# One level of Strassen's products in the two channel mixers of a decoder trunk in fp32

## The chip, the cores and the metric

One core of one Trainium2 chip runs the whole trunk in a single launch. The engines are TensorE (PE: matrix products into PSUM; its weight loads are listed as PEld), VectorE (DVE), ScalarE (ACT), GpSimd (POOL) and SyncE (SP), which here only issues transfers. The metric is the time of one execution in microseconds, the median of three runs.

## What is computed

A trunk of two layers over 512 tokens of width 1024. Layer 0 has a chunked gMLP mixer, layer 1 a gated linear recurrence; each is followed by the same channel mixer, a gated ConvFFN with inner width 3072. All in float32.

```
def conv_ffn(h, w_up, conv_w, conv_b, w_down):
    up = causal_dwconv(h @ w_up, conv_w, conv_b)
    gate, val = jnp.split(up, 2, axis=-1)
    return (jax.nn.gelu(gate) * val) @ w_down

def reference(x, ...):
    for i in range(DEPTH):
        h = rms_norm(x, norm_mix[i])
        ...
        x = x + mixer_a(...)          # layer 0; mixer_b in layer 1
        h = rms_norm(x, norm_ffn[i])
        x = x + conv_ffn(h, f_w_up[i], f_conv_w[i], f_conv_b[i], f_w_down[i])
    return rms_norm(x, norm_final)
```

`w_up` is 1024 x 6144 (3072 gate columns, 3072 value columns), `w_down` 3072 x 1024, the convolution has three causal taps over the tokens.

## The kernel before

**Layout.** Everything is feature-major: a tile has 128 features on the partitions and the 512 tokens along the free dimension. x stays in SBUF (`xall`, eight such rows, `xs[k]`). `out` is written transposed.

**Precision.** Every fp32 operand of a product is split into two parts in the format fp32r, hi (a rounded copy, made by ScalarE) and lo (the rest, a subtraction on VectorE), and each product of two tiles is three matmuls: hi·hi, hi·lo and lo·hi (`mm3`, lines 99 to 103). The splits of the weights stand in `split` (lines 85 to 91), with raised priority.

**Products.** `block` (lines 106 to 118) fills four PSUM banks, one for each of four blocks of 128 output features. It walks over the inner dimension in chunks of 256: a chunk is 512 KB of weights (128 x 2 x 512), loaded by SP into one of three `raw` buffers, split into one of three `hi` and one of three `lo` buffers, and multiplied in 2 x 4 x 3 = 24 matmuls of 512 columns. `hooks` put the norm's statistics between chunks; the norm's scale `rbc` is applied to the product's output.

**The channel mixer** (`conv_ffn`, lines 450 to 478). The up product runs in 12 groups of four chunks; a group gives two 128-feature tiles of the gate and the two value tiles that belong to them. Each of these four is multiplied by `rbc` out of PSUM (line 468), goes through three taps (`conv`, lines 442 to 448: one on ScalarE, two on VectorE), the gate tile through gelu, and the two are multiplied on VectorE (line 473) and split by `to_parts` into one of 24 kept pairs. The down product follows, two blocks of 12 chunks: `project` (adds to x, prepares the next norm) in layer 0, `project_out` (final norm, output by halves of the tokens) in layer 1. That makes 48 + 24 = 72 chunks of 24 matmuls in a mixer.

**Order.** The tile framework sets the order on each engine when the program is built, by readiness in its own model and by priority; within an engine instructions then run in that order. GpSimd has 19 instructions in the whole program: constants, four selections that cut the triangle of the spatial weights (line 397), and powers (`rsqrt_mean`, lines 210 to 213, and line 175).

Of the kernel before, what the change touches and what calls it, by code (L numbers as in the profile page):

```python
# [8 lines left out]
F32 = mybir.dt.float32  # L9
# [11 lines left out]
AG = 8  # L21
# [9 lines left out]
# Columns of the packed per-channel vectors.  # L31
# [13 lines left out]
def trunk(ctx: ExitStack, tc: tile.TileContext, xT, vecs, a_w_in, a_w_sT, a_b_s, a_w_out,  # L45
# [5 lines left out]
    yp = ctx.enter_context(tc.tile_pool(name="yp", bufs=24))  # L51
    wk = ctx.enter_context(tc.tile_pool(name="wk", bufs=7))
# [4 lines left out]

    def work(name="w"):
        return wk.tile([P, S], F32, tag="w", name=name)

    def work_r(name="wr"):
        return wk.tile([P, S], F32R, tag="w", name=name)

    def yhi(name="yh"):
        return yp.tile([P, S], F32R, tag="yh", name=name)

    def ylo(name="yl"):
        return yp.tile([P, S], F32R, tag="yl", name=name)

    # Activations whose tables differ, in the order of the program.  # L70
# [13 lines left out]
    # A chunk of a weight: 1024 values a partition, in two parts that add up to it exactly.  # L84
# [20 lines left out]
    # Feature-major product: one PSUM tile for each of four blocks of 128 output features.  # L105
    def block(kt, loader, acts, name, hooks={}):
        pss = [psum(f"{name}{m}") for m in range(4)]
        for kc in range(kt // 2):
            hi, lo = loader(kc)
            last = kc == kt // 2 - 1  # L110
            order = [(k, m) for m in range(4) for k in range(2)] if last else [(k, m) for k in range(2) for m in range(4)]
            for k, m in order:
                kk = 2 * kc + k
                w = (hi[:, k, m * P:(m + 1) * P], lo[:, k, m * P:(m + 1) * P])
                mm3(pss[m], w, acts[kk], kk == 0, kk == kt - 1)
            for hook in hooks.get(kc, ()):
                hook()
# [22 lines left out]
    # Keeps the tensor engine's clock up while the first loads are under way.  # L140
# [19 lines left out]
    # log of the sigmoid, by log1p(u) = 2 atanh(u / (2 + u)) with u = exp(-|lambda|)  # L160
# [36 lines left out]
    def norm_input(k, gain, ts=slice(None)):  # L197
        nc.scalar.activation(xh[k][:, ts], xs[k][:, ts], AF.Copy, scale=gain)  # L198
# [429 lines left out]
```

## Time and profile before

| | us |
|---|---|
| median of three runs | 1341.12 |
| the runs | 1341.08 to 1341.90 |
| span of the profiled execution | 1339.3 |
| PE busy in it | 1329.0 |
| DVE / ACT / POOL busy | 802.6 / 554.0 / 12.0 |
| transfers: mean busy share of the 16 engines, bytes | 29.7%, 129 MB |

The span runs from the first to the last instruction of the program. Busy times are unions of an engine's instructions; matmuls overlap, so the distance between their starts tells what one costs, not the listed duration. A row of a timeline has the start, the length, the engine, the source line, the operation, the tile written and the tiles read; "x3" means that so many equal instructions in a row are merged.

### The profile page before, as it was taken

How to read it: one execution, taken by the hardware profiler on the slowest of the kernel's cores; microseconds unless marked ns; L12 is line 12 of the kernel's file. 1: busy time of each engine (PE TensorE's matmuls, PEld its weight loads, DVE VectorE, ACT ScalarE, POOL GpSimd, SP SyncE). 2: the span in 40 equal slices, each digit the busy share in tenths (PEclk: the TensorE clock that was granted, in tenths of full speed). 3: DMA queues.
4: the chain of work that ended last, by engine and by line, in shares of the span. 5: the costliest groups of instructions: out<-in, count | busy, mean ns of one | idle time of the engine just before them, and what ended most of it. 6: DMA issues, size and time to landing. Idle time of an engine off the chain costs nothing.

```text
span 1339.3 us, 15007 instructions
## 1 busy us (share of the span) xinstructions
PE 1329.0 (99%) x5862; PEld 1082.5 (81%) x5862; DVE 802.6 (60%) x1104; ACT 554.0 (41%) x743; POOL 12.0 (1%) x20
## 2 busy tenths in 40 slices
PE   9999999999999999999999999999999999999997
PEld 7888888888888888888888888888888888888886
DVE  7227775446767575724247799944676757572325
ACT  6455332333434343423233669633343434342322
POOL 1000000000000000000000000000000000000000
PEclk9999999999999999999999999999999999999999
DMA  6333222232222222232233323232222222223221
GB/s 230 94 94 109 80 79 94 94 95 94 94 95 90 94 90 92 94 105 98 94 94 95 95 79 95 97 108 94 95 94 95 90 94 90 92 93 105 99 79 64
DMA packets 96328, 129.19 MB, mean 96 GB/s; under 512 B 5888, under 2 KB 61184, under 8 KB 96256
## 3 DMA queue, kind: packets, MB, share of 16 engines
q1 hardware_dynamic: 96112, 128.22, 29.7%
q8 instruction: 46, 0.75, 0.2%
q14 instruction: 26, 0.21, 0.1%
q10 hardware_dynamic: 144, 0.00, 0.0%
HBM read 126.11 MB, written 2.10 MB: 96 GB/s over the span
## 4 chain that ended last, share of the span: by engine, by line
PE 98%; issue 0%; DMA 0%; DVE 0%; ACT 0%; DVEq 0%; POOLq 0%; POOL 0%
PE f L101 13%; PE f L102 13%; PE f L103 13%; PE fd0p L102 3%; PE fd0p L103 3%; PE fd0p L101 3%; PE fd1p L101 3%; PE fd1p L102 3%; PE fd1p L103 3%; PE u L101 2%; PE v L362 2%; PE v L363 2%; PE u L103 2%; PE u L102 2%; PE v L364 2%; PE aop L101 2%
## 5 line engine op out<-in xcount | busy, mean ns | idle before, releaser
L446 DVE SCALAR_TENSOR_TENSOR cv<-up,vt,cv 128x511 f32<-128x511 f32 (+1 forms) x192 | 140.8, 745 | 22.2 <-ACT cv L444 21.3
L444 ACT ACTIVATE cv<-up,vt 128x512 f32<-128x512 f32 x96 | 77.7, 812 | 77.3 <-DVE up L468 77.3
L468 DVE TENSOR_TENSOR up<-f,rbc 128x512 f32<-128x512 f32 x96 | 65.4, 683 | 0.2 <-issue 0.2
L473 DVE TENSOR_TENSOR cv<-cv 128x512 f32<-128x512 f32 x48 | 33.0, 688 | 1.0
L472 ACT ACTIVATE cv<-cv 128x512 f32<-128x512 f32 x48 | 30.2, 629 | 5.5 <-DVE cv L446 3.3
L198 ACT ACTIVATE xh<-xall,vt 128x512 fp32r<-128x512 f32 x24 | 17.2, 719 | 23.8 <-DVE xall L250 23.8
L422 DVE SCALAR_TENSOR_TENSOR sv<-sv,vt,bs 128x256 f32<-128x256 f32 x32 | 14.9, 477 | 19.1 <-PE sv L419 19.1
L207 ACT ACTIVATE sq<-xall 128x512 f32<-128x512 f32 (+1 forms) x37 | 21.7, 586 | 9.8 <-DVE xall L262 9.8
L446 DVE SCALAR_TENSOR_TENSOR xb<-xr,vt,xb 128x511 f32<-128x511 f32 (+2 forms) x36 | 25.5, 744 | 0.1
L208 DVE TENSOR_TENSOR acc<-acc,sq 128x512 f32<-128x512 f32 (+1 forms) x37 | 23.8, 642 | 2.0 <-ACT sq L207 1.9
L199 DVE SCALAR_TENSOR_TENSOR xl<-xall,vt,xh 128x512 fp32r<-128x512 f32 x24 | 17.9, 748 | 5.2 <-ACT xh L198 4.8
L213 POOL TENSOR_TENSOR rc<-ms,mhalf 128x4 f32<-128x4 f32 (+1 forms) x6 | 5.4, 905 | 1233.5 <-DVE ms L212 1233.5
L418 PE MATMUL sv<-ws,vh 128*128 128x256 f32 x64 | 15.4, 324 | 0.0
L424 DVE SCALAR_TENSOR_TENSOR sv<-sv,vt 128x256 f32<-128x256 f32 x32 | 15.0, 480 | 0.4
L419 PE MATMUL sv<-ws,vl 128*128 128x128 f32 x64 | 14.2, 222 | 0.0
L559 DVE TENSOR_TENSOR_SCAN hs<-riyh,sq 128x512 f32<-128x512 f32 x12 | 14.0, 1205 | 0.0
L76 ACT ACT_TABLE_LOAD x10 | 12.8, 1283 | 0.1
L419 PEld LDWEIGHTS sv<-ws,vl 128*128 128x128 f32 x64 | 12.2, 191 | 0.5
L418 PEld LDWEIGHTS sv<-ws,vh 128*128 128x128 f32 x64 | 12.1, 188 | 0.5
L437 ACT ACTIVATE u<-u 128x512 f32<-128x512 f32 x16 | 9.4, 625 | 7.1 <-DVE u L436 7.1
L444 ACT ACTIVATE xb<-xr,vt 128x512 f32<-128x512 f32 x12 | 9.8, 814 | 6.1 <-DVE xr L492 6.1
L388 DVE SCALAR_TENSOR_TENSOR vl<-vr,rv,vh 128x512 fp32r<-128x512 f32 x16 | 10.9, 747 | 1.9 <-ACT vh L387 1.9
(2590 smaller groups left out, 4210.9 us busy)
## 6 DMA issues: line engine op xcount, KB each, us to landing
xall<-xT SPq DMA_DIRECT2D x8, 256.0 KB, 5.0
outT<-o SPq DMA_DIRECT2D x8, 256.0 KB, 2.4
av00raw<-a_w_in SPq DMA_DIRECT2D x2, 256.0 KB, 3.7
av01raw<-a_w_in SPq DMA_DIRECT2D x2, 256.0 KB, 4.9
av02raw<-a_w_in SPq DMA_DIRECT2D x2, 256.0 KB, 5.7
av03raw<-a_w_in SPq DMA_DIRECT2D x2, 256.0 KB, 5.2
bs<-a_b_s SPq DMA_DIRECT2D x1, 512.0 KB, 6.0
av10r<-a_w_in SPq DMA_DIRECT2D x1, 512.0 KB, 6.5
```

The costliest lines, as they stand in the source:

```text
L101: nc.tensor.matmul(ps, wh, xh, start=first, stop=False)
L102: nc.tensor.matmul(ps, wh, xl, start=False, stop=False)
L103: nc.tensor.matmul(ps, wl, xh, start=False, stop=last)
L362: nc.tensor.matmul(pss[c], xh[kk][:, ts], hi[:, k, :], start=kk == 0, stop=False)
L363: nc.tensor.matmul(pss[c], xh[kk][:, ts], lo[:, k, :], start=False, stop=False)
L364: nc.tensor.matmul(pss[c], xl[kk][:, ts], hi[:, k, :], start=False, stop=kk == KD - 1)
L418: nc.tensor.matmul(ps[:, i], vh[:, ds_], w, start=True, stop=False)
L444: nc.scalar.activation(dst, src, AF.Identity, scale=col(wname, woff + last * wstep), bias=col(cname, coff))
L446: nc.vector.scalar_tensor_tensor(dst[:, i:], src[:, :S - i], col(wname, woff + (last - i) * wstep), dst[:, i:], op0=ALU.mult, op1=ALU.add)
L468: nc.vector.tensor_tensor(upt, pss[2 * half + j], rbc, op=ALU.mult)
L472: nc.scalar.activation(ts[0], ts[0], AF.Gelu_apprx_tanh)
L473: nc.vector.tensor_tensor(ts[1], ts[0], ts[1], op=ALU.mult)
```

## The change

Each channel mixer's products are computed with one level of Strassen's scheme (seven products in place of eight), over quarters: the inner dimension is taken in pairs of 128-row blocks, the output features in two halves (gate and value for the up product; the lower and the upper 512 features of the width for the down product), and the tokens in two halves of 256.

- A chunk is again 512 KB of weights, four quarters of 128 x 256. `weight_sums` makes four sums of quarters in place (on GpSimd: one instruction of 512 elements and two of 256) and splits the seven combinations into two halves `j` of 7 x 128 columns, so two hi parts (ScalarE) and two lo parts (VectorE) of 896 elements in a chunk. There are three `hi` and three `lo` buffers as before, now of 7 x 128 columns, and two `raw` buffers (three before).
- `input_sums` makes the same kind of sums of the product's input (three GpSimd instructions), one cast of 1792 elements and one subtraction of 1792; for x once in a mixer per pair of rows (`prepare`, where gain and `rbc` now go into the input), for y in each group (`finish`).
- `seven` multiplies a chunk in 7 x 2 x 3 = 42 matmuls of 256 columns into seven of the eight PSUM banks.
- A group's seven banks are put together in `shared` and `up`: two copies on ScalarE, five instructions on VectorE (each reads one PSUM bank), two on GpSimd. The product of gate and value moves from VectorE to GpSimd.
- The down product runs in four chunks of the inner dimension, after the groups 3, 6, 8 and 11 (3, 3, 2 and 4 pairs, each for two halves of the output), and is added to x each time: four GpSimd instructions and seven on VectorE per product.
- The first group (`up_plain`, q = 0) keeps the old form, while the norm's statistics are made.
- The output is no longer sent by halves: the final norm follows the last product as a whole.
- SBUF pools are opened and closed by phase; x's parts `xparts` and six of the y tiles share a pool `top`; the first recurrent block takes its chunks in the order 0, 2, 1, 3. Comments are gone.

```
-    yp = ctx.enter_context(tc.tile_pool(name="yp", bufs=24))
-    wk = ctx.enter_context(tc.tile_pool(name="wk", bufs=7))
+    top = ctx.enter_context(tc.tile_pool(name="top", bufs=2))
...
+    PRODUCTS = ((1, 0, 0), (2, 2, 1), (6, 5, 5), (7, 3, 4), (5, 4, 3), (4, 1, 6), (3, 6, 2))
+    def weight_sums(src, name):
+        raw = wp.tile([P, 8, 256], F32, tag="raw", name=f"{name}r", bufs=2)
+        for k in range(2):
+            nc.sync.dma_start(raw[:, 2 * k:2 * k + 2], src[:, k])
+        parts = []
+        with tc.high_priority(HIGH):
+            nc.gpsimd.tensor_tensor(raw[:, 4:6], raw[:, 1:3], raw[:, 0:1].broadcast_to([P, 2, 256]), op=ALU.add)
+            nc.gpsimd.tensor_tensor(raw[:, 6], raw[:, 1], raw[:, 5], op=ALU.add)
+            nc.gpsimd.tensor_tensor(raw[:, 7], raw[:, 3], raw[:, 6], op=ALU.add)
+            for j in range(2):
+                cs = slice(j * P, (j + 1) * P)
+                hi = wp.tile([P, 7, P], F32R, tag="hi", name=f"{name}h{j}", padded_shape=[P, 8, P])
+                lo = wp.tile([P, 7, P], F32R, tag="lo", name=f"{name}l{j}", padded_shape=[P, 8, P])
+                nc.scalar.copy(hi, raw[:, 1:8, cs])
+                nc.vector.tensor_tensor(lo, raw[:, 1:8, cs], hi.bitcast(F32), op=ALU.subtract)
+                parts.append((hi, lo))
+        return parts
+    def input_sums(raw, dst):
+        nc.gpsimd.tensor_tensor(raw[:, 3:5], raw[:, 0:3:2], raw[:, 7:8].broadcast_to([P, 2, HS]), op=ALU.subtract)
+        nc.gpsimd.tensor_tensor(raw[:, 5], raw[:, 3], raw[:, 2], op=ALU.add)
+        nc.gpsimd.tensor_tensor(raw[:, 6], raw[:, 5], raw[:, 1], op=ALU.subtract)
+        hi, lo = dst[:, :, 0:HS], dst[:, :, HS:S]
+        nc.scalar.copy(hi, raw[:, 0:7])
+        nc.vector.tensor_tensor(lo, raw[:, 0:7], hi.bitcast(F32), op=ALU.subtract)
+    def seven(pairs, weight, name):
+        banks = {b: psum(f"{name}m{b}").rearrange("p (j t) -> p j t", j=2) for b, _, _ in PRODUCTS}
+        for n, (q, x) in enumerate(pairs):
+            parts = weight_sums(weight(q), f"{name}{q}")
+            first, last = n == 0, n == len(pairs) - 1
+            for b, w, i in PRODUCTS:
+                for j in range(2):
+                    hi, lo = parts[j]
+                    for m, (wt, xt) in enumerate(((lo, x[:, i, 0:HS]), (hi, x[:, i, 0:HS]), (hi, x[:, i, HS:S]))):
+                        nc.tensor.matmul(banks[b][:, j], wt[:, w], xt, start=first and j == 0 and m == 0,
+                                         stop=last and j == 1 and m == 2, skip_group_check=True)
+        return banks
+    def shared(banks, name):
+        e1, u2, u3 = (etile(f"{name}{t}") for t in ("e1", "u2", "u3"))
+        nc.scalar.copy(e1, banks[1])
+        nc.vector.tensor_tensor(u2, banks[6], e1, op=ALU.subtract)
+        nc.vector.tensor_tensor(u3, u2, banks[7], op=ALU.subtract)
...
+        def finish(q, gate, val):
+            nc.scalar.activation(gate, gate, AF.Gelu_apprx_tanh)
+            raw = yraw(f"yr{q}")
+            for j, place in enumerate(places(raw)):
+                nc.gpsimd.tensor_tensor(place, halves(gate[:, j]), halves(val[:, j]), op=ALU.mult)
...
+        def up(q):
...
+                nc.vector.tensor_tensor(val[:, :, 0:HS], banks[2], e1, op=ALU.add)
+                e5 = etile(f"f{q}e5")
+                nc.scalar.copy(e5, banks[5])
+                nc.gpsimd.tensor_tensor(gate[:, :, HS:S], u3, e5, op=ALU.subtract)
+                nc.gpsimd.tensor_tensor(e5, u2, e5, op=ALU.subtract)
+                nc.vector.tensor_tensor(gate[:, :, 0:HS], u3, banks[4], op=ALU.subtract)
+                nc.vector.tensor_tensor(val[:, :, HS:S], banks[3], e5, op=ALU.subtract)
...
+        top_pairs = (2, 3, 6, 7, 9, 10)
+        up_plain(0)
+        for q in range(1, NF // 2):
+            up(q)
+            if q in (3, 6, 8):
+                down({3: [0, 1, 2], 6: [3, 4, 5], 8: [6, 7]}[q], None)
+        down([8, 9, 10, 11], next_norm)
```

How the order changes is seen at three places. In the names, `f04m5` is bank 5 of layer 0's group 4, `f043h0` and `f043l0` the hi and lo part, half 0, of that group's chunk 3, and `x73` the sums of x for pair 3; without buffer numbers `f051l` is a lo part of group 5, chunk 1, `f5u` an eviction tile, `cg` and `cv` gate and value after the taps. Line numbers of the change are those of the changed file.

VectorE, before, one group of the up product (`up` is the scaled product, `cv` the taps, `fy` the parts of y):

```order
L90 TENSOR_TENSOR fu080l<-fu080r,fu080h 128x1024
L90 TENSOR_TENSOR fu081l<-fu081r,fu081h 128x1024
L468 TENSOR_TENSOR up<-f_3424,rbc 128x512
L446 SCALAR_TENSOR_TENSOR cv<-up,vt,cv 128x511
L468 TENSOR_TENSOR up<-f_3426,rbc 128x512
L446 SCALAR_TENSOR_TENSOR cv<-up,vt,cv 128x510
L468 TENSOR_TENSOR up<-f_3425,rbc 128x512
```

VectorE, after, from the end of group 5 to the next group's second chunk:

```order
L428 TENSOR_TENSOR f053l_4130<-f053r,f053h_4129 128x896
L428 TENSOR_TENSOR f060l_4228<-f060r,f060h_4227 128x896
L428 TENSOR_TENSOR f060l_4232<-f060r,f060h_4231 128x896
L469 TENSOR_TENSOR f5u_4178<-f05m_3946,f5e_4177 128x512
L543 TENSOR_TENSOR uv_4176<-f05m_3945,f5e_4177 128x2x256
L470 TENSOR_TENSOR f5u_4179<-f5u_4178,f05m_3947 128x512
L548 TENSOR_TENSOR ug_4175<-f5u_4179,f05m_3949 128x2x256
L549 TENSOR_TENSOR uv_4176<-f05m_3950,f5e_4184 128x2x256
L402 SCALAR_TENSOR_TENSOR cg_4190<-ug_4175,vt,cg_4190 128x511
L428 TENSOR_TENSOR f061l_4284<-f061r,f061h_4283 128x896
```

Where one lo part of 1024 stood per chunk there are now two of 896, and both lo parts of the next group's first chunk stand ahead of the five evictions.

GpSimd, after, in the same group (before, it has nothing in this stretch):

```order
L422 TENSOR_TENSOR f052r<-f052r 128x256
L511 TENSOR_TENSOR yr_3935<-cg_3920,cv_3927 128x2x256
L420 TENSOR_TENSOR f053r<-f053r 128x512
L511 TENSOR_TENSOR yr_3935<-cg_3920,cv_3927 128x512
L421 TENSOR_TENSOR f053r<-f053r 128x256
L434 TENSOR_TENSOR yr_3935<-yr_3935 128x512
L422 TENSOR_TENSOR f053r<-f053r 128x256
L435 TENSOR_TENSOR yr_3935<-yr_3935 128x256
```

The sums of the weights and of y are interleaved; there are 660 such additions and products in the program, 324 of 512 elements and 336 of 256.

TensorE, after, the end of a chunk and the start of the next group (a chunk before is eight times `hi`, `hi`, `lo` with 512 columns):

```order
L458 MATMUL f04m5_3678<-x73_2446,f043l1_3860 128x256
L458 MATMUL f04m5_3678<-x73_2446,f043h1_3859 128x256 x2
L458 MATMUL f04m4_3679<-x73_2446,f043l0_3856 128x256
L458 MATMUL f04m4_3679<-x73_2446,f043h0_3855 128x256 x2
L458 MATMUL f04m4_3679<-x73_2446,f043l1_3860 128x256
L458 MATMUL f04m4_3679<-x73_2446,f043h1_3859 128x256 x2
L458 MATMUL f04m3_3680<-x73_2446,f043l0_3856 128x256
L458 MATMUL f04m3_3680<-x73_2446,f043h0_3855 128x256 x2
L458 MATMUL f04m3_3680<-x73_2446,f043l1_3860 128x256
L458 MATMUL f04m3_3680<-x73_2446,f043h1_3859 128x256 x2
L458 MATMUL f05m1_3944<-x70_2419,f050l0_3958 128x256
```

Half 0 is used for the last time three matmuls before a chunk's end, and the next chunk's half 1 takes over its buffer.

## Rows read from the trace of the kernel before

**Rows 1.** The page: span, busy time by engine, chain that ended last.

```profile
span 1339.3 us, 15007 instructions
...
PE 1329.0 (99%) x5862; PEld 1082.5 (81%) x5862; DVE 802.6 (60%) x1104; ACT 554.0 (41%) x743; POOL 12.0 (1%) x20
...
PE 98%; issue 0%; DMA 0%; DVE 0%; ACT 0%; DVEq 0%; POOLq 0%; POOL 0%
```

**Rows 2.** Stages: both channel mixers, what follows, and one up group.

```profile
core 0: us, PE busy (x) PEld busy (x) DVE busy (x) ACT busy (x) POOL busy (x), PEclk, DMA share, GB/s
288.50:690.30 401.80, 401.80 (x1739) 326.38 (x1738) 229.72 (x293) 148.35 (x185) 1.01 (x1) 1.00 0.29 95
924.70:1328.50 403.80, 403.80 (x1798) 330.14 (x1797) 231.19 (x303) 150.48 (x193) 1.70 (x2) 1.00 0.27 88
1328.50:1339.30 10.80, 1.92 (x11) 1.23 (x10) 5.00 (x10) 0.93 (x2) 0.70 (x1) 0.70 0.57 195
...
309.00:331.40 22.40, 22.40 (x97) 17.99 (x97) 14.95 (x21) 9.33 (x12) 0.00 (x0) 1.00 0.29 94
```

**Rows 3.** Timeline of PE, start and length in us: 512 columns, then 256.

```profile
309.99 0.40 PE L103 MATMUL f<-xh,fu003l 128*128 128x512 f32 x1
310.22 0.40 PE L101 MATMUL f<-xh,fu003h 128*128 128x512 f32 x1
310.46 0.39 PE L102 MATMUL f<-xl,fu003h 128*128 128x512 f32 x1
...
1317.06 0.28 PE L101 MATMUL fd1p<-fy20h,fd1w110h 128*128 128x256 f32 x1
1317.18 0.28 PE L102 MATMUL fd1p<-fy20l,fd1w110h 128*128 128x256 f32 x1
1317.30 0.28 PE L103 MATMUL fd1p<-fy20h,fd1w110l 128*128 128x256 f32 x1
```

**Rows 4.** Groups of VectorE, 309 to 579 us: count, busy us, mean ns, idle before.

```profile
L446 DVE SCALAR_TENSOR_TENSOR cv<-up,vt,cv 128x511 f32<-128x511 f32 x48 | 35.7, 746 | 10.6 <-ACT cv L444 10.6
L468 DVE TENSOR_TENSOR up<-f,rbc 128x512 f32<-128x512 f32 x48 | 32.7, 683 | 0.0
L473 DVE TENSOR_TENSOR cv<-cv 128x512 f32<-128x512 f32 x24 | 16.5, 688 | 0.5
L90 DVE TENSOR_TENSOR fu032l<-fu032r,fu032h 128x1024 fp32r<-128x1024 f32 x1 | 1.2, 1226 | 0.0
```

**Rows 5.** Timeline of GpSimd and VectorE at 75 us.

```profile
75.51 0.41 POOL L397 TENSOR_SCALAR_AFFINE_SELECT wsm<-wsr 128x256 f32<-128x256 f32 x1 [45.12 <-DMA wsr<-a_w_sT]
75.87 1.39 POOL L397 TENSOR_SCALAR_AFFINE_SELECT wsm<-wsr 128x256 f32<-128x256 f32 x1
77.22 0.40 POOL L397 TENSOR_SCALAR_AFFINE_SELECT wsm<-wsr 128x256 f32<-128x256 f32 x1
75.60 1.40 DVE L90 TENSOR_TENSOR av32l<-av32r,av32h 128x1024 fp32r<-128x1024 f32 x1 [4.38 <-ACT av32h L89]
```

**Rows 6.** Groups of GpSimd, the whole span.

```profile
L175 POOL TENSOR_TENSOR lu<-ebase,nabs 128x12 f32<-128x12 f32 x1 | 2.3, 2279 | 18.6 <-DVE nabs L174 18.6
L213 POOL TENSOR_TENSOR rv<-ms,mhalf 128x4 f32<-128x4 f32 x1 | 1.0, 1008 | 5.2 <-DVE ms L212 5.2
masks.py:199 POOL TENSOR_SCALAR_AFFINE_SELECT ident<-ident 128x128 f32<-128x128 f32 x1 | 0.3, 293 | 0.0
```

**Rows 7.** ScalarE's casts: duration in ns; then a group as in rows 4.

```profile
L240 ACT CAST fy2h<-cv x2: 622/622/622, 339.4 to 975.6; 128x512 fp32r<-128x512 f32 x2
...
L89 ACT CAST fu030h<-fu030r 128x1024 fp32r<-128x1024 f32 x1 | 1.1, 1052 | 0.3 <-PE f L102 0.3
```

**Rows 8.** Transfers of weights: KB each, median us from issue to landing.

```profile
fu020r<-f_w_up SPq DMA_DIRECT2D x2, 256.0 KB, 3.0
```

**Rows 9.** Timeline of the end: the last product, the last scaling of the output.

```profile
1328.53 0.36 PE L103 MATMUL fd1p<-fy23h,fd1w111l 128*128 128x256 f32 x1
...
1332.91 2.48 DVE L288 TENSOR_TENSOR o<-xall,rb 128x512 f32<-128x512 f32 x4 [0.79 <-PE rb L285]
```

**Rows 10.** Timeline of PE at the start, ten matmuls in bf16.

```profile
1.26 4.19 PE L145 MATMUL warm<-warm 128*128 128x512 bf16 x10 [1.26 <-DVE warm L142]
```

More of the change, by code (lines that the diff above doesn't have):

```diff
@@ L56, in psum, with enter, keep, big @@
         return pp.tile([P, S], F32, tag="ps", name=name)
+    phase = {}
+    def enter(*pools):
+        stack = ExitStack()
+        for name, bufs in pools:
+            phase[name] = stack.enter_context(tc.tile_pool(name=name, bufs=bufs, reuse_waits="tile"))
+        return stack
     def work(name="w"):
-        return wk.tile([P, S], F32, tag="w", name=name)
+        return phase["wk"].tile([P, S], F32, tag="w", name=name)
     def work_r(name="wr"):
-        return wk.tile([P, S], F32R, tag="w", name=name)
+        return phase["wk"].tile([P, S], F32R, tag="w", name=name)
+    def keep(tag, name, dt=F32):
+        return phase["yp"].tile([P, S], dt, tag=tag, name=name)
     def yhi(name="yh"):
-        return yp.tile([P, S], F32R, tag="yh", name=name)
+        return keep("yh", name, F32R)
     def ylo(name="yl"):
-        return yp.tile([P, S], F32R, tag="yl", name=name)
+        return keep("yl", name, F32R)
+    def big(shape, name):
+        return top.tile(shape, F32R, tag="big", name=name)
     last_act = []
@@ L103, in mm3, with block @@
         nc.tensor.matmul(ps, wl, xh, start=False, stop=last)
-    def block(kt, loader, acts, name, hooks={}):
+    def block(kt, loader, acts, name, hooks={}, chunks=None):
         pss = [psum(f"{name}{m}") for m in range(4)]
-        for kc in range(kt // 2):
+        for n, kc in enumerate(chunks or range(kt // 2)):
             hi, lo = loader(kc)
-            last = kc == kt // 2 - 1
+            last = n == kt // 2 - 1
             order = [(k, m) for m in range(4) for k in range(2)] if last else [(k, m) for k in range(2) for m in range(4)]
@@ L114, in block @@
                 w = (hi[:, k, m * P:(m + 1) * P], lo[:, k, m * P:(m + 1) * P])
-                mm3(pss[m], w, acts[kk], kk == 0, kk == kt - 1)
-            for hook in hooks.get(kc, ()):
+                mm3(pss[m], w, acts[kk], n == 0 and k == 0, last and k == 1)
+            for hook in hooks.get(n, ()):
                 hook()
@@ L138, in load_x @@
         nc.sync.dma_start(xs[k], xT[k * P:(k + 1) * P, :])
+    mixer = enter(("yp", 24), ("wk", 5), ("bs", 1))
+    bs = phase["bs"].tile([P, AG, P], F32, name="bs")
+    new_x("xa")
     warm = work("warm").bitcast(BF16)[:, 0:S]
@@ L481, in trunk @@
+    mixer.close()
+    conv_ffn(0, "norm_mix", KD, None)
+    mixer = enter(("yp", 24), ("wk", 5))
     log_sigmoid()
```

233 lines of the change are left out of this document (125 added, 108 removed).

## The prediction

> **What bounds the kernel now.** I read the page first, then the stages, then single instructions. The page leaves one candidate: TensorE (PE) is busy 99% of 1339.3 us and holds 98% of the chain that ended last [rows 1]. The stages say the same of the part that the change touches. The two channel mixers' products run from 288.5 to 690.3 us and from 924.7 to 1328.5 us, 401.8 + 403.8 = 805.6 us, with PE busy throughout at a granted clock of 1.00, while VectorE (DVE) is busy for 57% and GpSimd (POOL) for 1 to 2 us [rows 2]. Everything else, the last 10.8 us included, is 1339.3 - 805.6 = 533.7 us. So the question is whether PE still sets the end when the other engines get more to do.
>
> **PE's part.** A 512-column matmul starts 0.23 us after the one before; a 256-column one, with its own weight load, 0.12 us [rows 3]. Before, a chunk (24 matmuls of 512) takes 24 x 0.232 = 5.57 us, 72 chunks a mixer. Now 4 chunks stay as they were (22.3 us) and 68 have 42 matmuls of 256: 42 x 0.12 = 5.04 us. If PE set the time, a mixer's matmuls would fall from 401 to 365 us, both by 72 us.
>
> **What the other engines get.** Per `up` group (four chunks, PE 20.2 us, before 22.3):
> DVE: a subtraction of 1024 takes 1.226 us, one of 512 about 0.685, a tap 0.745 [rows 4], so about 1.06 ns an element: 1.09 us for 896 and 2.04 us for 1792. Eight lo parts 8.7, eight taps 6.0, the lo of y 2.0, five evictions 3.4: 20.1 us, where a group before had 14.95 busy [rows 2]. DVE alone is level with PE.
> POOL: 9 sums of 512 and 10 of 256 (4 x (1+2) for the weights, 2 in the eviction, 2 products, 3 for y). No trace row shows an addition there. The nearest rows are a selection that reads one tile: 0.293 us for 128 elements, 0.41 for 256 [rows 5, 6], that is 0.18 + 0.91 ns an element. At that price a group's sums take 9 x 0.64 + 10 x 0.41 = 9.9 us, my lower end. An addition reads two tiles; with two reads an element it is 1.11 us for 512 and 0.64 for 256, 16.4 us a group. I take this: what differs is the number of reads. The only two-input rows are powers, 1.01 us for 4 elements and 2.28 for 12 [rows 6], 0.16 us an element; a power is another computation, so they are no end for a sum. The upper end comes from the sharing below.
> The Trainium skill (GPSIMD Engine Reference, section 3.1) gives 4497 ns for an fp32 addition of 2048 elements; an estimate from it is 2.2 ns x 7168 = 15.7 us a group, and the forecast would be some 15 us lower. No run here shows it yet.
>
> **The step that decides: DVE and POOL do not run side by side.** At 75.5 us POOL makes three equal selections. The first takes 0.41 us, the third 0.40; the second, started while a DVE subtraction with both inputs in SBUF was under way, 1.39, ending 0.26 us after that subtraction. The subtraction itself took 1.40 us instead of 1.226, ending 1.08 us after the first selection did [rows 5, 4]. Each waited for the other to finish; only some 0.15 us of start-up overlapped.
> The Trainium skill (SBUF — State Buffer, "Who interferes with whom") states it as an exclusive lock: DVE instructions with two SBUF inputs against GpSimd instructions that read SBUF, while a DVE instruction with at most one SBUF input is free. By that rule the trace agrees (1.39 against 0.41 us), and the exemption for evictions, which no row shows, would be worth 5 x 0.685 = 3.4 us a group, 75 us in all.
> In an `up` group DVE's two-SBUF work (lo parts, taps, lo of y) is 16.7 us and POOL's 16.4: 33.1 us in a row. If all 36 starts overlap by 0.15 us, 27.7 us remain; if evictions too never run beside POOL, 36.5. Both exceed PE's 20.2 and the 22.3 of before. I take 31, since the order pieces put both engines' instructions at the same places all through a group, with DVE waiting in line besides: it must finish the next group's second lo part (which waits for ScalarE's cast, and that for PE's last use of a buffer) before it empties this group's banks. That is 11 x 31 = 341 us a mixer.
>
> **The `down` chunks** have less beside them: per chunk 2 x 1.09 on DVE, 1.11 + 2 x 0.64 = 2.39 on POOL, and POOL's four updates of x, 4.4 us per product of some three chunks. Shared, that is 5.1 to 6.05 us, about PE's 5.04, so here two loops count. Weights: three buffers each for hi and lo, two a chunk. The second lo of a chunk gets its buffer only when PE has three matmuls of the chunk before left, and is needed after 15 to 18 matmuls: 24 x 0.12 + 0.28 (one matmul's own time [rows 3]) + cast 0.94 (896 elements, between 0.62 for 512 and 1.05 for 1024) [rows 7] + 1.09 + some 0.2 in semaphores = 5.4 us at best. ScalarE's own work, some 15 us a group, stays below all of these. Raw weights: two buffers, refilled by SP in order, each load behind the last subtraction that reads its buffer: landing 3.0 us [rows 8], POOL 2.39, two casts and two subtractions 4.1, some 0.5 in hand-overs, 10 us for two chunks. Every subtraction or sum that meets the other engine adds up to 1 us. I take 6.0 us (5.4 to 6.6): 24 x 6.0 = 144 us.
>
> **The smaller terms.** Making the input's sums before the first Strassen group: rbc is there about 3 us before the plain block ends, but the first pair needs two taps, three POOL sums, a cast of 1.7 and a subtraction of 2.04, 7.5 us: 6 us of wait (4 to 10). Ends of the 8 `down` products: 0.8 us each, 6 (2 to 16). The end of the kernel: before, the last product starts at 1328.53 and all is out 10.8 us later, with half of the output ready early [rows 9]. After, POOL's last updates (2.2), squares and their sums (3), the statistics, the power (1.0), spreading (2.6), eight multiplications (6) and the last transfer stand in a row, some 18.5 us: +8. The next mixer's first inputs: +3. The pools by phase and the other order of chunks in the recurrent mixer add no instruction; I cost them at nothing: PE's matmuls hide them, and without that cover they cost a chunk, 5.6 us.
>
> **Sum.** A mixer: 22.3 + 6 + 341 + 144 + 6 = 519.3; both 1038.6; with 533.7 + 8 + 3 = 1583.3 us, against 1339.3. The median of the runs, 1341.12, lies 1.8 us above the profiled span, so 1585. Lower ends (27.7, 5.4, 4, 2): 2 x 462.6 + 541.7 = 1467. Upper ends (36.5, 6.6, 10, 16): 2 x 608.2 + 544.7 = 1761.
>
> **The rivals.**
> *Faster: sharing costs next to nothing.* POOL's sums fall into DVE's waits and evictions, and PE sets the time: 2 x (22.3 + 6 + 68 x 5.04 + 6) + 544.7 = 1299. With some 1.5 us of stall at each of 11 groups where the banks come free late, 1332. It decides if a group stays below 20.5 us. For it: DVE idles 43% before [rows 2], and the eviction work needs one SBUF port only. Against: the 33.1 us that must pass one after the other.
> *The weight buffers alone bind, about no change.* Every chunk takes 5.4 us: 2 x (28.3 + 68 x 5.4 + 6) + 544.7 = 1348. Same condition on the sharing.
> *POOL adds at the price of one read.* A group's shared work is 16.7 + 9.9 = 26.6, less overlap 21.2, not below DVE's 20.1 plus the late banks; at 24 us and 5.6 a chunk: 2 x (28.3 + 264 + 134 + 6) + 544.7 = 1409.
> *The clock falls.* PE would wait a third of the time. At the start, before its clock rises, ten 512-column matmuls take 4.19 us together [rows 10], 0.42 each: the lower level, 1.2 GHz. At that rate a chunk takes 9 us, all of them 2 x (28.3 + 68 x 9 + 6) + 544.7 = 1837. Against: a chunk still has 5 us of matmuls in 7.
> *The change does not do what it says* (fewer columns through PE): the order shows 42 matmuls of 256 in every chunk, so I give it no chance of its own.
>
> **How the numbers follow.** Forecast, DVE and POOL in turn: 0.78, 1585 us (1467 to 1761). POOL at one read: 0.09. Faster: 0.08. No change: 0.03. Clock: 0.02. Each of the last three keeps its sign; of the one-read case 0.01 falls within 0.2%, about what a measurement of this kernel can tell from no change. So faster 0.08, same 0.04, slower 0.88. The range 1420 to 1720 leaves out the faster cases, the lower half of the one-read case and the top of the forecast's.
>
> **What would show it.** Right: POOL's weight sums with a spread of durations, from 1.1 us up to over 2; DVE's 896-element lo parts well over 1.09 us on the mean; PE's idle time ended by DVE's lo parts; `up` groups of 28 to 36 us; `down` chunks of 5.4 to 6.6 us; PE's busy share near 80%. Wrong: lo parts at 1.09 us with POOL busy beside them, PE still at 95% or more, groups of 20 to 22 us. If POOL's sums of 512 take 0.65 us, the price was too high; if groups are long with lo parts undisturbed, it was the buffers or the banks.

## The result, and the profile after

The changed kernel takes 1748.02 us (median of 4 runs, 1746.48 to 1752.15) against 1341.51 before: 1.303 times as long, 95% interval 1.302 to 1.305. Slower, as forecast, but 163 us above the forecast of 1585 and 28 above the range's end of 1720. The profiled execution is 1744.8 us long.

The page of the changed kernel, part 1 (busy us, share of the span, instructions) and part 4 (the chain that ended last); they answer to [rows 1]:

```profile
span 1744.8 us, 21472 instructions
...
PE 1412.7 (81%) x8252; PEld 1272.2 (73%) x8252; DVE 1167.9 (67%) x1301; ACT 703.5 (40%) x884; POOL 855.6 (49%) x679
...
PE 34%; POOL 32%; DVE 16%; issue 7%; DMA 6%; ACT 4%; SPq 1%; POOLq 0%; DVEq 0%; ACTq 0%
```

TensorE held 98% of the chain; now it is one of three. No engine is full, which is the sign of a chain through several engines and not of one bound.

The stages, as in [rows 2] (start:end, length, busy us of each engine, granted clock, DMA share, GB/s): both mixers' products, then the end.

```profile
284.00:883.90 599.90, 446.87 (x2963) 421.19 (x2962) 408.53 (x390) 223.81 (x258) 420.62 (x329) 0.88 0.20 62
1120.50:1720.50 600.00, 446.94 (x2963) 422.31 (x2962) 405.29 (x385) 219.67 (x253) 420.06 (x329) 0.88 0.19 60
...
1720.40:1744.80 24.40, 3.41 (x13) 2.42 (x11) 13.14 (x23) 2.88 (x5) 4.14 (x4) 0.59 0.22 86
```

The mixers went from 805.6 to 1199.9 us, +394; all else from 533.7 to 544.9, +11. DVE and POOL together are busy for 829 us of a mixer's 600, so they overlap for 229 at least; but a stretched instruction counts as busy while it waits. The lo parts of line 428 take between 1.07 and 2.20 us, 1.40 in the mean (min, median and max in ns behind the count, first and last start in us):

```profile
L428 DVE TENSOR_TENSOR f010l<-f010r,f010h x2: 1078/1086/1093, 296.0 to 302.5; 128x896 fp32r<-128x896 f32 x2
L428 DVE TENSOR_TENSOR f011l<-f011r,f011h x2: 1607/1612/1617, 312.8 to 318.0; 128x896 fp32r<-128x896 f32 x2
...
L428 DVE TENSOR_TENSOR f020l<-f020r,f020h x2: 2175/2179/2183, 347.2 to 349.3; 128x896 fp32r<-128x896 f32 x2
```

The subtractions that read PSUM (line 469) don't stretch: all 38 take 0.67 to 0.69 us, 25 of them with GpSimd busy beside them for over 0.3 us:

```profile
L469 DVE TENSOR_TENSOR f1u<-f01m,f1e x1: 678/678/678, 351.4 to 351.4; 128x512 f32<-128x512 f32 x1
...
L469 DVE TENSOR_TENSOR f5u<-f05m,f5e x1: 683/683/683, 538.8 to 538.8; 128x512 f32<-128x512 f32 x1
```

Seen together, the timeline of ACT, DVE, POOL and PE inside the `up` group f05 (start and length in us, count; in brackets the idle time before and what ended it):

```profile
528.19 0.94 ACT L427 CAST f053h<-f053r 128x896 fp32r<-128x896 f32 x1 [6.94 <-POOL f053r L422]
...
529.16 1.43 DVE L428 TENSOR_TENSOR f053l<-f053r,f053h 128x896 fp32r<-128x896 f32 x1 [4.77 <-ACT f053h L427]
529.60 2.13 POOL L420 TENSOR_TENSOR f060r<-f060r 128x512 f32<-128x512 f32 x1
...
530.64 0.58 PE L458 MATMUL f05m<-x,f053l 128*128 128x256 f32 x1 [3.07 <-DVE f053l L428]
...
531.02 0.63 PE L458 MATMUL f05m<-x,f053h 128*128 128x256 f32 x2
...
531.39 2.23 DVE L439 TENSOR_TENSOR y<-yr,y 128x1792 fp32r<-128x1792 f32 x1 [0.81 <-ACT y L438]
...
531.81 2.40 POOL L421 TENSOR_TENSOR f060r<-f060r 128x256 f32<-128x256 f32 x1
...
533.54 1.62 DVE L428 TENSOR_TENSOR f053l<-f053r,f053h 128x896 fp32r<-128x896 f32 x1
...
534.03 0.40 PE L458 MATMUL f05m<-x,f053h 128*128 128x256 f32 x2
...
534.28 1.46 POOL L422 TENSOR_TENSOR f060r<-f060r 128x256 f32<-128x256 f32 x1
...
535.21 0.39 PE L458 MATMUL f05m<-x,f053l 128*128 128x256 f32 x1 [0.42 <-DVE f053l L428]
```

TensorE's wait of 3.07 us is for the first lo part of chunk f053. That one took 1.43 us, so most of the wait comes from earlier steps: the cast before it found ScalarE idle for 6.94 us, until the last of the chunk's GpSimd sums was done. Afterwards TensorE's pairs take 0.63 us instead of 0.40 for some 3 us, the lower of its two levels (1.2 GHz). The sharing is seen behind that: a sum of 256 elements (0.72 us undisturbed) started at 531.81 beside the y part and ended 0.6 us after it; the second lo part, in line behind the y part, took 1.62 us, and TensorE waited 0.42 us for it.

### The profile page after: what moved, and what is told of

Its sections match the earlier page's. It is cut to its first block, busy times and chain, and to the rows that moved or that the text cites. A ratio compares the mean times of both kernels' runs of the same rounds, so it can differ in the third digit from the quotient of the medians.

```text
span 1744.8 us, 21472 instructions
## 1 busy us (share of the span) xinstructions
PE 1412.7 (81%) x8252; PEld 1272.2 (73%) x8252; DVE 1167.9 (67%) x1301; ACT 703.5 (40%) x884; POOL 855.6 (49%) x679
## 4 chain that ended last, share of the span: by engine, by line
PE 34%; POOL 32%; DVE 16%; issue 7%; DMA 6%; ACT 4%; SPq 1%; POOLq 0%; DVEq 0%; ACTq 0%
POOL yr L511 4%; DVE cg L402 4%; POOL yr L434 2%; POOL ug L546 2%; PE u L115 2%; PE aop L115 2%; PE u L117 2%; PE aop L117 2%; PE aop L116 2%; PE u L116 2%; PE v L319 2%; PE v L320 2%; PE v L318 2%; DVE cv L402 1%; PE bop L117 1%
## 5 line engine op out<-in xcount | busy, mean ns | idle before, releaser
L511 POOL TENSOR_TENSOR yr<-cg,cv 128x512 f32<-128x512 f32 x44 | 77.4, 1763 | 61.8 <-DVE cv L402 54.6
L402 DVE SCALAR_TENSOR_TENSOR cv<-uv,vt,cv 128x511 f32<-128x511 f32 (+1 forms) x88 | 91.9, 1066 | 6.2 <-ACT cv L400 5.7
L402 DVE SCALAR_TENSOR_TENSOR cg<-ug,vt,cg 128x511 f32<-128x511 f32 (+1 forms) x88 | 89.8, 1060 | 0.1
L439 DVE TENSOR_TENSOR y<-yr,y 128x1792 fp32r<-128x1792 f32 x24 | 51.7, 2154 | 46.1 <-ACT y L438 46.1
L438 ACT CAST y<-yr 128x1792 fp32r<-128x1792 f32 x24 | 40.5, 1690 | 62.3 <-POOL yr L436 62.0
L400 ACT ACTIVATE cv<-uv,vt 128x512 f32<-128x512 f32 x44 | 34.9, 812 | 57.6 <-DVE cg L402 57.6
L400 ACT ACTIVATE cg<-ug,vt 128x512 f32<-128x512 f32 x44 | 34.5, 809 | 22.9 <-POOL ug L546 22.9
L434 POOL TENSOR_TENSOR yr<-yr 128x512 f32<-128x512 f32 x24 | 36.6, 1525 | 0.6
L439 DVE TENSOR_TENSOR x<-xr,x 128x1792 fp32r<-128x1792 f32 x8 | 16.7, 2091 | 13.5 <-ACT x L438 13.2
L231 DVE TENSOR_TENSOR acc<-acc,sq 128x512 f32<-128x512 f32 x35 | 24.0, 685 | 1.7 <-ACT sq L230 1.3
L435 POOL TENSOR_TENSOR yr<-yr 128x256 f32<-128x256 f32 x24 | 20.3, 847 | 0.8
L436 POOL TENSOR_TENSOR yr<-yr 128x256 f32<-128x256 f32 x24 | 19.2, 799 | 1.7
```

The costliest lines, as they stand in the source:

```text
L400: nc.scalar.activation(dst, src, AF.Identity, scale=col(wname, woff + last * wstep), bias=col(cname, coff))
L402: nc.vector.scalar_tensor_tensor(dst[:, i:], src[:, :S - i], col(wname, woff + (last - i) * wstep), dst[:, i:], op0=ALU.mult, op1=ALU.add)
L434: nc.gpsimd.tensor_tensor(raw[:, 3:5], raw[:, 0:3:2], raw[:, 7:8].broadcast_to([P, 2, HS]), op=ALU.subtract)
L438: nc.scalar.copy(hi, raw[:, 0:7])
L439: nc.vector.tensor_tensor(lo, raw[:, 0:7], hi.bitcast(F32), op=ALU.subtract)
L511: nc.gpsimd.tensor_tensor(place, halves(gate[:, j]), halves(val[:, j]), op=ALU.mult)
```

## The experiments

Theory A, from the prediction: VectorE and GpSimd take turns at SBUF, and that is nearly all of the loss. Rivals: B, the weight buffers and PSUM banks; C, the clock after a wait; D, the row of steps that each chunk goes through (transfer, three sums, two casts, two lo parts) and what stands ahead of them in the queues. Times are of single runs, beside which the kernel before took 1341 to 1342 us; runs of the changed kernel spread by 0.3%.

**Taking the sharing away.** The second operand of VectorE's lo parts, taps and y parts becomes a PSUM bank:

```diff
-nc.vector.tensor_tensor(lo, raw[:, 1:8, cs], hi.bitcast(F32), op=ALU.subtract)
+nc.vector.tensor_tensor(lo, hi.bitcast(F32), phase["pc"][:, 0:P].unsqueeze(1).broadcast_to([P, 7, P]), op=ALU.subtract)
...
-dst[:, i:], src[:, :S - i], col(wname, woff + (last - i) * wstep), dst[:, i:],
+dst[:, i:], (src if other is None else other)[:, :S - i], col(wname, woff + (last - i) * wstep), dst[:, i:],
...
+banks[3] = banks[4]
```

> Changed: in both channel mixers the second operand of VectorE's lo parts of the weights, of all convolution taps and of the lo parts of y and x is a zeroed PSUM bank instead of an SBUF tile; products 3 and 4 of each group of seven share one PSUM bank so that a bank is free for it (so the values computed are not the reference's). GpSimd does all the work that it did. Theory A (the two engines take turns at SBUF, which makes a mixer about as long as the sum of GpSimd's 327 us and VectorE's 270 us of two-read work, 597): nothing is left to take turns with, GpSimd's sums fall from 1.47 to 1.27 us in the mean and lo 896 from 1.40 to about 1.1, and a mixer falls from 600 us to between the PE work at the full clock (about 366) and 440, so the kernel to 1345 to 1430 us. Rival B (too few hi/lo, raw buffers or banks): these are as before, 1700 to 1760. Rival D (GpSimd is slow in itself and each weight chunk waits for its three sums in a row): the three sums last as long as GpSimd makes them, 1600 to 1700.

Measured 1979.85 us. Nearly every duration fell to its floor, and yet the kernel got slower by 232. The timeline at the start of group f08 says why:

```profile
739.10 1.68 ACT L438 CAST y<-yr 128x1792 fp32r<-128x1792 f32 x1 [6.10 <-POOL yr L436]
740.82 2.02 DVE L439 TENSOR_TENSOR y<-y,pconst 128x1792 fp32r<-128x1792 f32 x1 [6.03 <-ACT y L438]
742.75 2.08 DVE L428 TENSOR_TENSOR f080l<-f080h,pconst 128x896 fp32r<-128x896 f32 x2
...
743.98 0.56 PE L459 MATMUL f08m<-x,f080l 128*128 128x256 f32 x1 [20.42 <-DVE f080l L428]
```

The scheduler kept all readers of the one constant in program order, so the next group's lo parts stood behind this group's y part: TensorE waited 20 us a group. It tells nothing on sharing, but much on order. The control shows the PSUM side alone to cost little, 15 us, 1763.26:

> The control of e1: only the PSUM side of it, products 3 and 4 in one bank and one bank held, all operands as in the changed kernel (so the outputs are not the reference's). Theory A: 1735 to 1760, within 1% of the changed kernel. Rival B, if it is the banks: bank 3 comes free with bank 4 only, every group starts later, and the time moves by 20 us or more.

With the order edges between lo parts, taps and y parts removed, VectorE's order is close to the changed kernel's (some 170 of its 1301 instructions stand elsewhere, as some 140 do in the control):

```diff
+tc.declare_no_dep(ins.ins, group=f"pc{other}", query=mybir.DependencyQuery.ANY, reason="constant")
```

> As in the run with one SBUF operand (VectorE's lo parts, taps and y parts of both mixers read a zeroed PSUM bank as their second operand; products 3 and 4 share a bank; the values are not the reference's), but VectorE's order is the changed kernel's again: in that run each instruction that read the shared bank was queued in the order of the program, so the lo parts of a group stood behind the y part of the group before, and TensorE waited some 20 us at each of 22 groups. GpSimd does all its work. Theory A (turns at SBUF are the cost): durations are at their floor (lo 1.08, sums 1.27 and 0.72, taps 0.745) and a mixer is 400 to 470 us, the kernel 1345 to 1490. Rival D (the row of steps that a chunk and a y go through, and the order in which the queues take them, is the cost, contention or not): 1600 or more. Rival B (buffers): between, 1500 to 1650.

Measured 1588.73: 159 us less (174 against the control), 248 still above the kernel before. Lo 1.08 us, sums 1.30 and 0.745, taps 0.743: next to no sharing is left, and TensorE still waits. Theory A's 1345 to 1490 is refuted; the sharing is part of the loss, and alone the smaller one. The time lies in rival B's range and just under D's 1600.

The edit does a second thing. A lo part no longer reads the raw buffer, so SP may refill that after ScalarE's cast, and need not wait for VectorE. The longest waits of SP in the first mixer, of the changed and of the one-read kernel (us in total, times, longest):

```profile
SPq L417 <- DVE f030l L428: 17.5, 1, 17.5
...
SPq L425 <- ACT f020h L435: 14.8, 1, 14.8
```

So the 159 us are for the sharing and for a raw buffer that is free earlier, by 1.1 us or more a chunk (a lo part's length); no run here takes the two apart. GpSimd in that kernel, across two groups:

```profile
461.77 1.27 POOL L428 TENSOR_TENSOR f042r<-f042r 128x512 f32<-128x512 f32 x1
463.11 0.73 POOL L429 TENSOR_TENSOR f042r<-f042r 128x256 f32<-128x256 f32 x1
463.92 0.73 POOL L430 TENSOR_TENSOR f042r<-f042r 128x256 f32<-128x256 f32 x1
469.92 1.29 POOL L428 TENSOR_TENSOR f043r<-f043r 128x512 f32<-128x512 f32 x1 [5.26 <-DMA f043r<-f_w_up]
...
476.18 1.29 POOL L428 TENSOR_TENSOR f050r<-f050r 128x512 f32<-128x512 f32 x1 [3.33 <-DMA f050r<-f_w_up]
...
481.28 1.29 POOL L428 TENSOR_TENSOR f051r<-f051r 128x512 f32<-128x512 f32 x1 [2.17 <-DMA f051r<-f_w_up]
```

Undisturbed sums, and chunks 5.1 to 8.2 us apart: each time GpSimd waits for a transfer that could not start before a raw buffer was free. For chunk f043 the way back is seen. The second cast of f041 had waited 4.66 us until TensorE left a hi buffer; it ends at 465.93, and then the transfer into its raw buffer is issued:

```profile
464.99 0.94 ACT L435 CAST f041h<-f041r 128x896 fp32r<-128x896 f32 x1 [4.66 <-PE f04m L469]
...
466.02 1.20 SPq L425 DMA_DIRECT2D f043r<-f_w_up  x2
```

The hi buffers and the raw buffers, which the prediction priced as two loops, are links of one chain here.

**Sharing without Strassen.** The kernel before, with idle work for GpSimd on each `up` chunk:

```diff
+for a, b_ in ((r[:, 0, 0], r[:, 1, 0]), (r[:, 0, 1], r[:, 1, 0]), (r[:, 0, 1], r[:, 0, 0]), (r[:, 1, 1], r[:, 0, 0])):
+    nc.gpsimd.tensor_tensor(d, a, b_, op=ALU.add)
```

> The kernel before, with four GpSimd adds of 256 elements more on each weight chunk of the `up` products, whose result nobody reads: some 4 x 0.72 = 2.9 us of GpSimd in each chunk of 5.27 us, no Strassen, no other change. Theory A: the lo parts lengthen from 1.22 to 1.5 or more and the taps from 0.745 to 0.9 or more, the evictions (PSUM operand, 0.683) stay, and since 2.9 us and VectorE's 2.5 us of two-read work make about a chunk's 5.27 us, `up` gets longer: 1350 to 1420. Without sharing: durations as in the kernel before and 1341 within 5 us.

Measured 1345.61 against 1340.94. Busy times of one line each in the `up` stage of the first mixer (lo parts; taps; GpSimd's adds):

```profile
311.00:542.50 231.50, 60.41 (x41) 1.00 0.29 94
...
311.00:542.50 231.50, 83.80 (x83) 1.00 0.29 94
...
311.00:542.50 231.50, 182.59 (x164) 1.00 0.29 94
```

That is 1.47 us a lo part (1.226 in [rows 4]), 1.01 a tap (0.745), 1.11 an add (0.72); the multiplications out of PSUM in its timeline stay at 0.68. So the sharing is real without Strassen, but it costs this kernel 5 us: beside a TensorE that is busy throughout, the stretched instructions still end in time. The expected 1350 to 1420 was too much.

**Taking work off GpSimd.**

```diff
+nc.sync.dma_start(raw[:, 4 + 2 * k:6 + 2 * k], src[:, k])
...
-nc.gpsimd.tensor_tensor(raw[:, 4:6], raw[:, 1:3], raw[:, 0:1].broadcast_to([P, 2, 256]), op=ALU.add)
-nc.gpsimd.tensor_tensor(raw[:, 6], raw[:, 1], raw[:, 5], op=ALU.add)
-nc.gpsimd.tensor_tensor(raw[:, 7], raw[:, 3], raw[:, 6], op=ALU.add)
```

> Left out: the three GpSimd sums on each weight chunk of the mixers; their four places are filled by a second load of the same quarters, so VectorE, ScalarE and TensorE do what they did on other numbers, and the transfers double. GpSimd keeps the sums of x and y, the gating product, two eviction sums a group and the adds into x. Theory A: 68 chunks x (1.27 + 2 x 0.72) = 184 us a mixer leave the common time, 597 - 184 = 413, more than the PE work of 366 by little, so the kernel falls by 2 x 160 to 2 x 184, to 1380 to 1430. Rival C (the lowered TensorE clock after stalls is what costs, port or not): a clock near 0.88 stays and the time is 1500 or more. Rival B: the raw buffer is free earlier, but hi/lo and banks are as before, 1600 to 1700.

Measured 1578.42, 170 us less where theory A wanted 320 or more. Rival C's "1500 or more" holds, with a granted clock of 0.91 in the first mixer. The two that move sums to VectorE, computing the same (the first every sum of the mixers in this way, the second the three on the weights):

```diff
-nc.gpsimd.tensor_tensor(raw[:, 6], raw[:, 1], raw[:, 5], op=ALU.add)
+nc.vector.tensor_tensor(raw[:, 6], raw[:, 1], raw[:, 5], op=ALU.add)
```

> All of the mixers' GpSimd sums on VectorE instead (what is computed stays the same). Theory A: no second engine at SBUF; VectorE's own work is about 325 us a mixer at the floor durations and 162 x 0.685 + 168 x 0.41 = 180 more, 505, so it is the bound in place of 600: 1540 to 1600. If GpSimd's work had been beside VectorE's for nothing, moving it to the busier engine would make the kernel slower: over 1760.

> Only the three sums on each weight chunk on VectorE, the rest stays on GpSimd (what is computed stays the same). Theory A: two-read work 270 + 68 x (0.685 + 2 x 0.41) = 372 on VectorE and 143 on GpSimd take turns, 515 of 600: 1560 to 1620. Rival D (the row of steps in a chunk): the three sums take 1.5 us instead of 2.7 in each chunk, and y keeps GpSimd for itself, so it would fall as far or further: 1450 to 1560.

Measured 1609.3 and 1724.03. All on VectorE is a little above its forecast (VectorE is then at 81% of the span). Nothing is shared in that run either, while the raw buffers still wait for the lo parts, and it gains 139 us; its sums are shorter too. With only the weights' sums on VectorE the gain is 24 us, neither theory's number: these sums now stand in VectorE's queue and still take turns with GpSimd's work on y.

**Clock.** Eight idle matmuls behind each chunk of the control:

```diff
+with tc.issue_after(mm.ins):
+    for _ in range(8):
+        nc.tensor.matmul(phase["pc"], zero[:, 0:P], zero, start=True, stop=True)
```

> To the control with a shared and a held bank (1763) come eight matmuls of 512 columns on zeros into the held bank after each chunk of the mixers, some 1.8 us of TensorE that nobody uses, where it otherwise waits for the next chunk's lo part (a chunk takes 8.5 us, its own matmuls 5.05). Rival C (TensorE comes out of each wait at its lower clock, 0.21 us a matmul instead of 0.12, and that is part of the loss): the granted clock rises from 0.90 towards 0.97 and the time falls to 1660 to 1740. If the clock only follows the waits: 1755 to 1800.

Measured 1863.93, above both expected ranges, with the clock up from 0.901 to 0.937. Some 136 x 1.8 = 245 us of idle matmuls cost 101; whether the rest fell into waits or was paid back by the clock, this run can't tell. It shows that filling the waits does not pay, and not that the lower clock costs nothing. TensorE is busy for 446.9 us in a mixer whose matmuls would take 365 at the prices of [rows 3], and for 374.6 us in the kernel with all three cuts below. By this estimate the lower level adds up to 82 us a mixer. It comes after waits and lengthens the chain in turn; what part of the loss it makes is not separated.

**Buffers, banks and their order.** Five hi, five lo and three raw buffers, their room taken from two prepared inputs:

```diff
-stack = enter(("x7", 4), ("y", 2), ("up", 3), ("ee", 3), ("yr", 1))
+stack = enter(("x7", 2), ("y", 2), ("up", 3), ("ee", 3), ("yr", 1), ("wx", 2), ("wr", 1))
```

> Five hi and five lo buffers instead of three and three raw buffers instead of two for the seven products' weights, all else as in the changed kernel. Their room comes from two of the four prepared inputs, which are neither prepared nor kept: groups 2 and 3 of the input features read those of 0 and 1 (so the outputs are not the reference's). Theory A: the sum of the work that takes turns is what it was, less two preparations of some 6 us a mixer: 1715 to 1745. Rival B: with nearly twice the buffers TensorE no longer waits for the chunk, 1400 to 1550.

Measured 1664.75, between both: 83 us less, of which 22 at most are the preparations left out (the first Strassen groups, f01 and f11, take 11.4 and 10.7 us less). Two edits of order, which compute the same:

```diff
-for b, w, i in PRODUCTS:
-    for j in range(2):
+steps = [(j, p) for p in PRODUCTS for j in range(2)] if last else [(j, p) for j in range(2) for p in PRODUCTS]
+for j, (b, w, i) in steps:
```

> Of each weight chunk but a group's last, TensorE does all 21 matmuls of the first half (hi and lo of 128 columns) before the 21 of the second; in the changed kernel the first half's last matmul stands some 3 to 6 places before the chunk's end, so that its buffers come free only there. Same instructions, same results. Theory A (turns at SBUF): the shared work is the same, 1720 to 1748. Rival B (the three hi and lo buffers): a buffer comes free 2 us earlier in each of some 100 chunks, 1550 to 1650.

> Both at once: VectorE's second operands of both mixers in PSUM (the values are not the reference's; order as in the changed kernel), and the first half's 21 matmuls before the second's. With turns at SBUF gone the kernel was at 1589, 248 us above the kernel before, and TensorE still waits. If what is left there is the hi and lo buffers: 1400 to 1480. If it is the row of steps of a chunk (transfer 3.5, three sums 2.8, two casts 1.9, the lo parts 2.2) through two raw buffers, and other instructions ahead of them in the queues: 1540 to 1590.

Measured 1749.35 and 1552.67: nothing while the sharing is there, 36 us without it, which is inside the 1540 to 1590 expected for the row of steps. VectorE's additions out of the banks ahead of GpSimd's four into x at the end of each `down` product:

```diff
-nc.gpsimd.tensor_tensor(x1[:, :, t0], x1[:, :, t0], e1, op=ALU.add)
...
 nc.vector.tensor_tensor(x1[:, :, t0], banks[2], x1[:, :, t0], op=ALU.add)
...
+nc.gpsimd.tensor_tensor(x1[:, :, t0], x1[:, :, t0], e1, op=ALU.add)
...
```

> Only the order of nine additions at the end of each `down` product is changed: VectorE's five, which empty the PSUM banks, come before GpSimd's four into x, instead of behind them. The sums are the same. If TensorE waits there for banks (in the changed kernel a product of three chunks takes some 25 us, its matmuls 15): 3 to 5 us at each of 16 products, 1670 to 1700. If its wait there is for lo parts and y, which share SBUF: 1735 to 1755.

Measured 1726.58: 21 us, less than half of the 48 to 78 expected for banks. TensorE's waits for these additions, some 25 us in all in the changed kernel, are gone in this one.

**The three cuts together.** The edits above, combined: the one-read kernel without the weight sums, the same with more buffers, with both, and the changed kernel with more buffers and without the weight sums.

> Two cuts at once: VectorE's second operands of both mixers in PSUM, in the changed kernel's order (alone: 1589), and the three GpSimd sums on each weight chunk left out, their places filled by a second load (alone: 1578). Alone they are worth 159 and 170 us of the 407. If they are two things, turns at SBUF and a row of GpSimd steps in each chunk's way, both together give 1400 to 1440. If they are two views of one (what the first removes is mostly what the weight sums cause), the second adds little: 1520 to 1575.

> The one-read kernel (VectorE's second operands of the mixers in PSUM; 1589) with five hi, five lo and three raw buffers, for which two of the four prepared inputs are left out (so values are not the reference's; some 12 us less work a mixer). In the changed kernel these buffers were worth 84 us, of which some 20 is the left out work. If what is left at 1589 is each chunk's row of steps through two raw and three hi/lo buffers: 1400 to 1470. If it is GpSimd's own 327 us a mixer in line and the ends of the products: 1530 to 1570.

> The same with the three GpSimd sums of each weight chunk left out too (their places filled by a second load): no turns at SBUF, no weight sums, more buffers. Without the buffers this was 1488. If buffers are what is left: 1360 to 1400, near the 1299 that the matmuls alone would give. If the ends of the products and the starts of the mixers are: 1440 to 1470.

> More buffers (two of four prepared inputs left out) and no weight sums (second load in their places), with VectorE's operands in SBUF as in the changed kernel, so GpSimd's sums for y, the evictions and x still meet it. If the three cuts add up, 1748 less 83 and 170 is 1495. If sharing is mostly the weight sums meeting the lo parts, it is now near the 1340 of all three: 1350 to 1400.

All eight combinations, us:

| | as changed | one SBUF read |
|---|---|---|
| nothing else | 1748.0 | 1588.7 |
| more buffers | 1664.8 | 1491.5 |
| no weight sums | 1578.4 | 1487.7 |
| both | 1484.7 | 1340.5 |

Read as differences: the sharing is worth 91 to 173 us depending on what else is there, the weight sums 101 to 180, the buffers 83 to 147. Each cut takes more with it than its name says: the one-read kernels also free the raw buffers earlier and give up a bank; without the weight sums there is less for VectorE to share with; the kernels with more buffers also leave out half of the input's preparation, up to 22 us. So the table weighs these edits, not pure causes. None is enough alone: alone they are worth 159, 170 and 83 us, sharing and weight sums together 260 and not 329, and the last of the three 144 to 151, whichever it is. Of the four expectations for combinations three missed: 1491.5 and 1487.7 lay between the two expected, 1340.5 below both; 1484.7 came near the 1495 of two cuts added up. Only with all three gone do the `up` groups run near TensorE's pace, 20.16 to 22.1 us after the first, and the page reads

```profile
span 1338.4 us, 20910 instructions
...
PE 1267.0 (95%) x8252; PEld 1161.7 (87%) x8252; DVE 983.9 (74%) x1291; ACT 688.8 (51%) x880; POOL 290.5 (22%) x259
...
PE 56%; DVE 23%; POOL 14%; issue 4%; ACT 2%; DMA 0%; POOLq 0%; DVEq 0%; ACTq 0%
```

And that is 1340.5 us, the time of the kernel before, for a kernel that leaves out the weight sums and half of the preparation. Even then a mixer is 399 us long from its first product (284.0 to 682.9 us), since the first Strassen group waits for the input's sums and the last two `down` products for y, lo parts and the banks (27.6 us for f01; 30.4 and 20.4, from end to end, for d080 and d081, whose matmuls take 20.2). No run here points to a Strassen version that beats the kernel before.

## Why the prediction was right and wrong

**The direction** was right, and so was its ground: PE's 72 us of saved matmuls don't count once other engines set the pace.

**GpSimd's price** was 12% too low. A sum of 512 takes 1.26 us at least and one of 256 0.72, not 1.11 and 0.64; a group's sums 9 x 1.27 + 10 x 0.72 = 18.6 us, not 16.4. The Trainium skill's GPSIMD Engine Reference, section 3.1, is right per element (2.2 ns; these sums differ by 2.1 ns an element); the estimate made from it, 15.7 us a group, left out the 0.18 us that each of 19 instructions takes besides.

**Taking turns** is as [rows 5] showed it, and the exemption for one SBUF input, which no row of before showed, holds: 38 subtractions of line 469 between 673 and 692 ns. Here the trace agrees with the Trainium skill, SBUF — State Buffer, "Who interferes with whom".

**An `up` group** was put at 31 us; the 22 took 34.3 in the mean (28.2 to 40.0), in all 753.6 us against 682 and 12 for the first ones' wait: +60. The full row at measured prices, 18.6 + 16.7 = 35.3, fits better than my 31. But that fit misleads: with next to nothing left to share, a group still takes 28.5 us (313.8 for the first mixer's 11).

**A `down` chunk** was put at 6.0 us; it took 8.2 (197.6 us for the first mixer's 24, 196.5 for the second's). With the 6 for ends, 150 were forecast: +94 for both mixers, the largest miss; the plain first groups, 26.0 us up to the first Strassen matmul instead of 22.3, are the last 7 of the 161. The step that failed is "have less beside them", and the sharing is the smaller part of it: in the one-read kernel a chunk still takes 7.6 us (182 for the first mixer's 24). The taps, gating and y sums of the last group run beside `down`, and they stand in the queue ahead of its weight sums. GpSimd's timeline at the end of the first `down` product:

```profile
438.47 1.65 POOL L511 TENSOR_TENSOR yr<-cg,cv 128x512 f32<-128x512 f32 x1 [4.21 <-DVE cv L402]
440.08 1.73 POOL L420 TENSOR_TENSOR d0012r<-d0012r 128x512 f32<-128x512 f32 x1
441.77 2.19 POOL L511 TENSOR_TENSOR yr<-cg,cv 128x512 f32<-128x512 f32 x1
443.93 0.72 POOL L421 TENSOR_TENSOR d0012r<-d0012r 128x256 f32<-128x256 f32 x1
444.62 1.28 POOL L434 TENSOR_TENSOR yr<-yr 128x512 f32<-128x512 f32 x1
445.87 0.73 POOL L422 TENSOR_TENSOR d0012r<-d0012r 128x256 f32<-128x256 f32 x1
```

The weight sums of chunk d0012, 2.7 us at their floor, are done 8.1 us after the first of these rows starts, since each waits for a y sum in between, and the first of those for VectorE's taps.

**The rivals' common premise** is the deeper fault. Forecast less "faster" is 1585 - 1332 = 253 us: some 205 for the turns in the `up` groups, 46 for `down` chunks at 6.0 us instead of 5.04. The one-read cut is worth 159 in all. That "PE sets the time" once the sharing costs nothing (1299 to 1332) failed by over 250: the one-read kernel takes 1589. The loops were worked out at their best, 5.4 us for the hi and lo buffers and 10 for two chunks through the raw ones, with nothing queued ahead of any step, and compared with the others as if the longest alone counted. The runs fit a sum instead: each step is late by what stands before it on its engine, and two raw buffers carry the delay to the next transfer, as the rows of f043 and d0012 show. How the sum divides among the steps is not shown. In the `up` groups the shared time took the place of that missing term and hid it, which is luck.

**The small terms** came out in sum, by luck: 544.9 us for all outside the mixers against 533.7 + 11 = 544.7. The end is 24.4 us instead of 18.5, the stage between the mixers 236.6 instead of 234.4, and the first mixer starts 4.5 us earlier, which was not forecast.

**The clock** fell after waits (0.88 in the mixers), as its rival said, but to nothing like one level throughout; 1837 was not it. The forecast itself had no term for a lower clock, and TensorE is busy up to 82 us a mixer longer than it was priced; how much of the 163 us above the forecast that makes stays open.

**The range.** The forecast's own upper end, 1761, held the result; the stated range left out its top, from 1720 on. The misses of `up` and `down` had the same sign.

## What to carry to other kernels

An engine's instructions that stretch beside another's cost time only where they stand in the path that sets it: measure it with idle work in the old kernel (5 us here) and without it in the new one (159), before putting a loss on it, and ask what else the edit frees. When a chunk passes through four engines on two or three buffers, work out its whole row of steps, with what is queued ahead of each, and don't take the longest loop for the sum. Moving work to an idle engine buys little when the work stands in the path of every chunk and its queue also holds instructions that wait for others.

## What the runs showed of the hardware

GpSimd's fp32 addition of two SBUF tiles: 1.26 us for 512 elements and 0.72 for 256, so some 0.18 + 2.1 ns an element; VectorE does the same in 0.685 and 0.417 (the run with all sums there). Beside each other a sum of 256 took up to 2.6 us and a lo part of 896 up to 2.2 instead of 1.08. Not expected: with its second operand in PSUM VectorE's lo part of 896 is as long as with both in SBUF (1.08 us); two reads from SBUF cost nothing more by themselves, only beside GpSimd.
